# Hybrid attention encoder layer: VectorE jobs made by late ScalarE jobs run a slot later; the mixed rows' squares and low parts within VectorE's budget

## The chip, the cores and the metric

One core of one Trainium2 chip. The metric is the device time of one execution in microseconds (us), smaller is better. A core has TensorE (PE, matrix products; PEld is its weight load), VectorE (DVE), ScalarE (ACT), GpSimd (POOL) and SyncE (SP), each with its own queue that runs in order. Engines wait for each other through semaphores.

## The reference, cut to what matters

The layer reads x of 1024 tokens by 1024 columns. One projection of the normalised x gives queries, keys, values and gates of two groups of heads. Group A is plain attention, group B looks at a neighbourhood on a token grid of 16 rows by 64 columns. Both are gated, put beside each other, projected again and added to x.

```python
h = _rmsnorm(x, norm_gain[l])
proj = h @ w_in[l]
q_a, k_a, v_a, g_a, q_b, k_b, v_b, g_b = jnp.split(proj, split_at, axis=-1)
...
o_a = _gqa_blocked(q_a, k_a, v_a) * jax.nn.silu(g_a)
o_b = _neighbourhood_attn(q_b..., k_b..., v_b..., na_rpb[l])
o_b = o_b * jax.nn.silu(g_b)
mixed = jnp.concatenate([o_a, o_b], axis=-1)
x = x + mixed @ w_out[l]
return _rmsnorm(x, final_norm_gain)
```

The result is float32. The kernel gets near that precision with float16 products by splitting each operand into a high part (rounded to float16) and a low part (what is left), and adding three products: high by high, high by low, low by high.

## The kernel before

**Stages.** First x is normalised, split and transposed (to about 74 us). Then come projections and group A's attention in one loop of units (to about 366 us). Then group B's attention runs in 32 steps, four for each block u of 128 tokens and two heads a step; meanwhile PE also runs the rest of the gate projections and the first part of the output projection. After that the rest of the output projection and the last norm follow, without steps of attention.

**A step of group B** (`fl.step`, called by `run_units`, with `parts_b`). `b_lo` makes the low part of the previous step's probabilities (L845 on DVE) and issues their transpose on SP (L847). `b_qk` puts two heads' scores on PE (L815 and L818, into one of three score banks), takes for each the biased scores and their minimum on DVE (L836), two exponentials on ACT (L838) and a cast to the high part (L840). Then the jobs of DVE are emitted, then about 24 matmuls of projection on PE (`fill`, L494), and last `b_pv`, the product with the values of three steps earlier (L865 to L867). The order in which these calls are made is each engine's order, as the engines are scheduled by hand there.

**Jobs.** Everything else of ACT and DVE is a job. `job(engine, cost, fn, delay, late)` puts one into a list with a first step at which it may run and a class `late`; `work(engine)` takes jobs in the order of (late, first step, number) as long as the engine's budget for the step holds out. A job with `late=0` runs whatever the budget is. `fl.step` calls `work("act")` twice: ahead of `b_qk` for at most 1.2 us of cost (`fl.early`, set only in group B's loop), and behind it for the rest ("late ACT jobs"); `work("dve")` comes behind both. `need` runs jobs at once, out of turn, when PE is about to use their result.

**The jobs that matter here.**
- *Weights.* `load_w(g)` fetches the 1 MB of group g's weights (L212, on POOL's queue). Four steps later `squares` adds up their squares in quarters on ACT (L362); two steps after that PE sums them over the partitions (L378, in `b_scores`), DVE scales the sum (L380) and POOL takes a power (L381). `split` then makes four ACT jobs `hi` (L404) and, from each, a DVE job `lo` (L409, called `wlo` here, group by group). The last `lo` of group g lets group g+2 be loaded at the next step. Groups 13 to 16 are the output projection.
- *Mixed rows.* When a block u has all its heads, `os_start` runs: squares on ACT (`sq`, L902) and then DVE (`scale`, L907), a power on POOL (L910), two ACT jobs `hi` (L915) and two DVE jobs `lo` (L919), and two transposes on SP (L928). These are ready for the output projection.
- *Gates.* The tanh is an ACT job (L694), the product behind it a DVE job (L699); both are made at once, when the projection ends.
- *Values.* DVE divides by the sums (L874 to L877), POOL multiplies by the gate (L879). The output projection is added to x by L976; L1001 squares the result for the last norm.

Of the kernel before, what the change touches and what calls it, by code (L numbers as in the profile page):

```python
# [47 lines left out]
class Flow:  # L48


    def __init__(self):
        self.slot = 0
        self.due = {}
        self.queue = []
        self.credit = 0.0
        self.jobs = []
        self.base = None
        self.budget = {}
        self.left = {}
        self.early = None  # L60

    def at(self, delay, pos, fn, *a):
        self.due.setdefault((self.slot + delay, pos), []).append((fn, a))

    def job(self, eng, cost, fn, *a, delay=1, late=1, key=None):

        self.jobs.append((late, self.slot + delay, self.number(), eng, cost, fn, a, key))

    def need(self, key, done):
# [50 lines left out]
    def step(self, n, first=None, second=None, last=None):  # L120
        if self.base:
            us = self.base[0] + 0.654 * n
            self.budget = {"act": us - self.base[1], "dve": us - self.base[2]}
        self.run("pre")
        self.work("act", self.early)
        if first:
            first()
        if self.early is not None:
            self.work("act", more=True)
        if second:  # L130
            second()
        self.run("mid")
        self.work("dve")
        self.run("post")
        self.fill(n)
        if last:
            last()
        self.run("end")
        self.slot += 1
# [3 lines left out]
def kernel(ctx: ExitStack, tc: tile.TileContext, x: bass.AP, w: bass.AP, wo: bass.AP,  # L143
# [3 lines left out]
    act, dve, pool, pe, sp = nc.scalar, nc.vector, nc.gpsimd, nc.tensor, nc.sync  # L147
# [11 lines left out]
    at, job = fl.at, fl.job  # L159
# [42 lines left out]
    def tn(name, n=1, tag="t"):  # L202
        return tiny.tile([P, n], F32, tag=tag, name=name)


    raw, wp, late, x2 = {}, {}, {}, {}
# [149 lines left out]
    def squares(g, delay):  # L356

        wss[g] = [tn(f"wss{g}_{k}", 1, "ws") for k in range(4)]

        def quarter(i):  # L360
            o = late["r"][0][:, 2048:2560].bitcast(BF16) if "b" in late else va_more
            act.activation(o.rearrange("p (k c) -> p k c", c=GC), raw[g][:, QUARTERS[i]], AF.Square, accum_out=wss[g][i])  # L362
            if i == 3:
                job("act", 0, pend.append, g, delay=2 if "b" in late else 1, late=0, key=("sq", g))
        for i in range(4):
            job("act", 0.75 if g < 13 else 1.0, quarter, i, delay=delay, late=3 if g < 13 else 1.2, key=("sq", g))
# [31 lines left out]
    def split(g):  # L398

        alloc_wp(g)  # L400

        def hi(i):
            q = QUARTERS[i]
            act.activation(wp[g][0][:, q], raw[g][:, q], AF.Copy, scale=col(S_ + g))  # L404
            job("dve", 1.0 if "b" in late else 0.72, lo, i, delay=0, late=0.5 if g > 11 else 2, key=g)

        def lo(i):
            q = QUARTERS[i]
            dve.scalar_tensor_tensor(wp[g][1][:, q], raw[g][:, q], col(S_ + g), wp[g][0][:, q], op0=OP.mult, op1=OP.subtract)  # L409
            if i < 3:  # L410
                return
            ready.add(g)
            prep_e(g)
            if g + 2 < 17:
                at(1, "pre", load_w, g + 2)
            if g > 14:
                t = wraw.tile([P, 2, 1024], F32, tag="raw", name=f"x2{g}")
                for i in range(2):
                    have_x2(ORDER[2 * g - 26 + i], t[:, i])
        for i in range(4):  # L420
            job("act", 0.3 if g == 14 else 0.6, hi, i, late=0.5 if g > 11 else 2, key=g)
# [464 lines left out]
    def mixed(u):  # L886
        return mixA[u // 2][:, u % 2], mixB[u // 2][:, u % 2]

    def os_start(u):

        if not all({("b", u, c), ("a", u // 2, c * GC)} <= ready for c in range(2)):
            at(1, "post", os_start, u)
            return
        t = rws[u] = tn(f"os{u}", 4, "os")
        k = ORDER.index(u)
        hl = one.tile([P, 2, 1024], F16, tag=f"q{k % 2}0" if k > 3 else "gain", name=f"mhl{u}")
        osp[u] = [hl[:, 0], hl[:, 1]]
        ms = mixed(u)
        cs = [slice(i * 512, (i + 1) * 512) for i in range(2)]

        def sq():
            act.activation(late["r"][0][:, 2048:2560].bitcast(BF16), ms[0], AF.Square, accum_out=t[:, 0:1])  # L902
            job("dve", 0.95, scale, delay=0, late=0, key=("os", u))

        def scale():
            junk = late["r"][1][:, 2048:2560] if k else osp[u][0][:, cs[1]]
            dve.tensor_tensor_reduce(out=junk.bitcast(BF16), in0=ms[1], in1=ms[1], scale=1.0, scalar=t[:, 0:1],  # L907
                                     op0=OP.mult, op1=OP.add, accum_out=t[:, 1:2])
            dve.tensor_scalar(t[:, 1:2], t[:, 1:2], 2.0 ** -30, 1e-36, op0=OP.mult, op1=OP.add)
            pool.tensor_tensor(t[:, 2:3], t[:, 1:2], mh[:, :1], op=OP.pow)  # L910
            for i in range(2):
                job("act", 0.72, hi, i, delay=1, late=0, key=("os", u))

        def hi(i):
            act.activation(osp[u][0][:, cs[i]], ms[i], AF.Copy, scale=t[:, 2:3])  # L915
            job("dve", 0.8, lo, i, delay=0, late=0, key=("os", u))

        def lo(i):
            dve.scalar_tensor_tensor(osp[u][1][:, cs[i]], ms[i], t[:, 2:3], osp[u][0][:, cs[i]], op0=OP.mult, op1=OP.subtract)  # L919
            if i:  # L920
                dve.reciprocal(t[:, 3:4], t[:, 2:3])
                os_c(u)
        job("act", 0.82, sq, delay=1, late=0, key=("os", u))

    def os_c(u):
        mT[u] = [m.bitcast(F16).rearrange("p (a b) -> p a b", b=P) for m in mixed(u)]
        for k in range(2):
            sp.dma_start_transpose(mT[u][k], osp[u][k])  # L928
        at(1, "end", turn_x2, u)
# [369 lines left out]
```

## Time and profile before

| what | us |
|---|---|
| median of 3 runs (567.64 to 570.32) | 567.69 |
| the profiled execution, device time | 566.36 |
| its span | 564.5 |
| PE busy | 515.5 (91%) |
| DVE busy | 446.0 (79%) |
| ACT busy | 367.8 (65%) |

The span runs from the first to the last instruction; the other 1.9 us lie around it. Group B's first scores start at 366.1 us and its last at 502.0. In rows of groups, "xcount | busy, mean ns | idle" gives how many instructions there were, their busy time, the mean of one in ns, and how long the engine had been idle ahead of them, with what ended the idle time. In rows of the timeline the first number is the start, the second the duration, both in us.

### The profile page before, as it was taken

How to read it: one execution, taken by the hardware profiler on the slowest of the kernel's cores; microseconds unless marked ns; L12 is line 12 of the kernel's file. 1: busy time of each engine (PE TensorE's matmuls, PEld its weight loads, DVE VectorE, ACT ScalarE, POOL GpSimd, SP SyncE). 2: the span in 40 equal slices, each digit the busy share in tenths (PEclk: the TensorE clock that was granted, in tenths of full speed). 3: DMA queues.
4: the chain of work that ended last, by engine and by line, in shares of the span. 5: the costliest groups of instructions: out<-in, count | busy, mean ns of one | idle time of the engine just before them, and what ended most of it. 6: DMA issues, size and time to landing. Idle time of an engine off the chain costs nothing.

```text
span 564.5 us, 13778 instructions
## 1 busy us (share of the span) xinstructions
PE 515.5 (91%) x5583; PEld 402.4 (71%) x5583; DVE 446.0 (79%) x911; ACT 367.8 (65%) x583; POOL 157.2 (28%) x181
## 2 busy tenths in 40 slices
PE   2577989989999999999999999999998889998994
PEld 0456877767887555568888888887776667788883
DVE  4588788989887988778789887588987798988532
ACT  5546456958787759587696886367777568663211
POOL 2395887670000000000000022433821231224000
PEclk9979999999999999999999999999999998999998
DMA  8999549789999999998999899436586599996612
GB/s 242 220 181 234 122 71 210 125 143 191 203 228 174 175 216 193 193 187 173 211 197 180 189 165 214 129 68 132 105 188 105 117 255 230 181 154 139 215 38 75
DMA packets 244513, 95.47 MB, mean 169 GB/s; under 512 B 235489, under 2 KB 236001, under 8 KB 242530
## 3 DMA queue, kind: packets, MB, share of 16 engines
q1 hardware_dynamic: 240850, 73.89, 71.8%
q0 software_dynamic: 3312, 19.92, 12.2%
q8 instruction: 43, 0.70, 0.5%
q10 hardware_dynamic: 288, 0.79, 0.5%
q14 instruction: 20, 0.16, 0.1%
HBM read 29.56 MB, written 4.19 MB: 60 GB/s over the span
## 4 chain that ended last, share of the span: by engine, by line
PE 51%; DVE 9%; ACT 8%; issue 5%; DMA 4%; SPq 0%; POOL 0%; DVEq 0%; POOLq 0%; ACTq 0%
PE pj L494 19%; PE kb L494 7%; PE pjb L494 5%; PE s L725 4%; PE s L727 4%; ACT rq L838 3%; PE sb L494 3%; PE pv L758 3%; DMA ar<-ar 3%; PE pv L759 3%; PE pv L757 3%; ACT ar L840 3%; DVE ar L836 2%; DVE ar L845 2%; DMA x2b<-in_x_dram 1%
## 5 line engine op out<-in xcount | busy, mean ns | idle before, releaser
L494 PEld LDWEIGHTS <-hT 128*128 128x128 f16 x2112 | 204.9, 100 | 58.8 <-issue 16.2
L494 PE MATMUL pj<-whl,hT 128*128 128x256 f16 x1680 | 201.6, 278 | 20.9 <-DMA hT<-ar 7.8
L734 ACT ACTIVATE ar<-s,nm,sm 128x1024 f32<-128x1024 f32 x64 | 76.9, 1202 | 56.6 <-DVE nm L732 56.3
L732 DVE CUSTOM_DVE_ANT_0 ar<-s,sm 128x1024 bf16<-128x1024 f32 x64 | 82.0, 1281 | 33.9 <-PE s L727 33.6
L494 PEld LDWEIGHTS <-ar 128*128 128x128 f16 x768 | 74.6, 99 | 11.7 <-issue 2.6
L740 DVE TENSOR_TENSOR ar<-ar 128x1024 f16<-128x1024 f32 x64 | 79.5, 1242 | 1.4 <-ACT ar L735 1.4
L735 ACT ACTIVATE ar<-ar 128x1024 f16<-128x1024 f32 x64 | 67.6, 1057 | 2.1 <-DVE sum L764 0.3
L838 ACT ACTIVATE rq<-ar,nm 128x384 f32<-128x384 f32 (+1 forms) x64 | 34.1, 580 | 38.4 <-DVE nm L836 37.7
L494 PE MATMUL pjb<-whl,ar 128*128 128x256 f16 x408 | 47.4, 273 | 0.0
L494 PE MATMUL kb<-hT,whl 128*128 128x512 f16 x192 | 44.5, 379 | 0.0
L409 DVE SCALAR_TENSOR_TENSOR whl<-raw,sm,whl 128x512 f16<-128x512 f32 x52 | 38.7, 770 | 2.8 <-ACT whl L404 2.8
L758 PE MATMUL pv<-va,ar 128*128 128x64 f16 x384 | 40.1, 194 | 0.0
L757 PE MATMUL pv<-va,ar 128*128 128x65 f16 x384 | 40.1, 193 | 0.0
L759 PE MATMUL pv<-va,ar 128*128 128x65 f16 x384 | 39.9, 192 | 0.0
L757 PEld LDWEIGHTS <-ar 128*128 128x128 f16 x384 | 35.7, 97 | 5.5 <-issue 0.3
L758 PEld LDWEIGHTS <-ar 128*128 128x128 f16 x384 | 35.5, 97 | 5.5 <-issue 0.3
L725 PE MATMUL s<-kTa,rq 128*128 128x512 f16 x128 | 38.5, 383 | 0.4 <-ACT ar L734 0.4
L212 POOL DMA_DIRECT2D raw<-in_w_dram x11 | 6.7, 607 | 113.0 <-ACT ar L735 89.0
L845 DVE SCALAR_TENSOR_TENSOR ar<-rq,ar 128x768 f16<-128x768 f32 (+1 forms) x32 | 30.7, 959 | 7.9 <-ACT ar L840 7.5
L879 POOL TENSOR_TENSOR ar<-ar,qkg 128x256 f32<-128x256 f32 x16 | 18.5, 1157 | 65.0 <-DVE qkg L877 63.7
L759 PEld LDWEIGHTS <-ar 128*128 128x128 f16 x384 | 35.5, 99 | 0.0
L404 ACT ACTIVATE whl<-raw,sm 128x512 f16<-128x512 f32 x52 | 34.0, 709 | 1.4 <-POOL sm L381 1.4
(174 smaller groups left out, 978.4 us busy)
## 6 DMA issues: line engine op xcount, KB each, us to landing
raw<-in_w_dram POOLq DMA_DIRECT2D x11, 1024.0 KB, 7.7
raw<-in_wo_dram POOLq DMA_DIRECT2D x4, 1024.0 KB, 6.3
ar<-in_x_dram SPq DMA_DIRECT2D x7, 512.0 KB, 6.3
khh<-ar SPq DMA_DIRECT2D x16, 128.0 KB, 3.4
x2b<-in_x_dram POOLq DMA_DIRECT2D x4, 512.0 KB, 6.9
x<-in_x_dram POOLq DMA_DIRECT2D x4, 512.0 KB, 6.2
out_dram<-x2b SPq DMA_DIRECT2D x8, 256.0 KB, 4.2
out_dram<-x SPq DMA_DIRECT2D x7, 256.0 KB, 2.9
```

The source lines that it names most:

```text
L409: dve.scalar_tensor_tensor(wp[g][1][:, q], raw[g][:, q], col(S_ + g), wp[g][0][:, q], op0=OP.mult, op1=OP.subtract)
L494: pe.matmul(*o[0], **o[1])
L725: pe.matmul(s[:, c * 512:(c + 1) * 512], q, kTa[:, 4 * c:4 * c + 4, hh], start=True, stop=False)
L732: dve.tensor_tensor_reduce(out=hl[:, 1].bitcast(BF16), in0=s, in1=col(SHA).to_broadcast([P, 1024]), scale=col(NSA), scalar=3e38, op0=OP.ad ...
L734: act.activation(p32, s, AF.Exp, bias=nm, scale=col(SCA))
L735: at(0, "mid", lambda: act.activation(hl[:, 0], p32, AF.Copy))
L740: dve.tensor_tensor(hl[:, 1], p32, hl[:, 0], op=OP.subtract)
L757: pe.matmul(o, pt[:, kt], va[:, kt, hh, v_hi], start=kt == 0, stop=False)
L758: pe.matmul(o[:, :D], pt[:, kt], va[:, kt, hh, v_lo], start=False, stop=False)
L759: pe.matmul(o, pt[:, 8 + kt], va[:, kt, hh, v_hi], start=False, stop=kt == 7)
L838: act.activation(p32[:, e], t[:, e], AF.Exp, bias=nm, scale=-1.0)
L845: dve.scalar_tensor_tensor(hl[:, 1], p32, 2.0 ** 14, hl[:, 0], op0=OP.mult, op1=OP.subtract)
```

## The change

A field `lag` holds how many steps later than the current one a new job may run at the earliest. It is 1 while late ACT jobs run and 0 otherwise, so that a job which a late ACT job makes (a DVE `lo` behind its `hi`, above all) can run in the next step at the earliest, and no longer in the same one. And three DVE jobs of the mixed rows are no longer of class 0: the squares `scale` and both `lo` get `late=0.2`, so they count against the budget and stand behind class 0; the cost given for `lo` goes from 0.8 to 0.95.

```diff
@@ class Flow
+        self.lag = 0
...
     def job(self, eng, cost, fn, *a, delay=1, late=1, key=None):
 
+        delay = max(delay, self.lag)
         self.jobs.append((late, self.slot + delay, self.number(), eng, cost, fn, a, key))
@@ def step
         if self.early is not None:
+            self.lag = 1
             self.work("act", more=True)
+            self.lag = 0
@@ def os_start
         def sq():
             act.activation(late["r"][0][:, 2048:2560].bitcast(BF16), ms[0], AF.Square, accum_out=t[:, 0:1])
-            job("dve", 0.95, scale, delay=0, late=0, key=("os", u))
+            job("dve", 0.95, scale, delay=0, late=0.2, key=("os", u))
...
         def hi(i):
             act.activation(osp[u][0][:, cs[i]], ms[i], AF.Copy, scale=t[:, 2:3])
-            job("dve", 0.8, lo, i, delay=0, late=0, key=("os", u))
+            job("dve", 0.95, lo, i, delay=0, late=0.2, key=("os", u))
```

No instruction is added or dropped; the order changes on ACT, DVE, POOL and SP, and on PE only in the place of the weights' sums. Line numbers of the changed kernel are 4 higher from `fl.step` on.

**ACT, steps 14 and 15.** Before, the exponentials and cast of step 14 (`nm_4`, `nm_5`) are followed by three quarters of group 15's squares and the mixed rows' `hi`, then by step 15 (`nm_6`, `nm_7`) and the tanh:

```order
L838 ACTIVATE rq<-ar,nm_4_5938 128x384
L838 ACTIVATE rq<-ar,nm_5_5941 128x384
L840 ACTIVATE ar<-rq 128x768
L362 ACTIVATE rest_5101,wss_0_5670<-raw_5668 128x512
L362 ACTIVATE rest_5101,wss_1_5671<-raw_5668 128x512
L362 ACTIVATE rest_5101,wss_2_5672<-raw_5668 128x512
L915 ACTIVATE mhl_5887<-ar,os_5886 128x512 x2
L838 ACTIVATE rq<-ar,nm_6_6008 128x384
L838 ACTIVATE rq<-ar,nm_7_6011 128x384
L840 ACTIVATE ar<-rq 128x768
L694 ACTIVATE ar<-pjb_5196,sm 128x512
```

The same place in the changed kernel, from the same exponentials to the same tanh:

```order
L842 ACTIVATE rq<-ar,nm_4_5930 128x384
L842 ACTIVATE rq<-ar,nm_5_5933 128x384
L844 ACTIVATE ar<-rq 128x768
L919 ACTIVATE mhl_5879<-ar,os_5878 128x512 x2
L842 ACTIVATE rq<-ar,nm_6_6005 128x384
L842 ACTIVATE rq<-ar,nm_7_6008 128x384
L844 ACTIVATE ar<-rq 128x768
L698 ACTIVATE ar<-pjb_5196,sm 128x512
```

The three squares are gone from here; they now stand in steps 18 and 19.

**DVE, steps 15 and 16.** Before, from the gate product and the sums of step 15 to the minima of step 16 (`nm_0`, `nm_1`) and the next squares:

```order
L699 SCALAR_TENSOR_TENSOR ar<-ar,pjb_5196 128x2x256
L874 RECIPROCAL sumb_1_6017<-pvb_5116 128x4
L875 TENSOR_TENSOR sumb_1_6017<-sumb_1_6017,sm 128x4
L877 TENSOR_TENSOR qkg<-pvb_5116,sumb_1_6017 128x256
L919 SCALAR_TENSOR_TENSOR mhl_5887<-ar,os_5886,mhl_5887 128x512 x2
L921 RECIPROCAL os_5886<-os_5886 128x1
L845 SCALAR_TENSOR_TENSOR ar<-rq,ar 128x768
L836 ISA ar,nm_0_6081<-sb_5113,ar,sm 128x384
L836 ISA nm_0_6081 128x1
L836 ISA ar,nm_1_6084<-sb_5111,ar,sm 128x384
L836 ISA nm_1_6084 128x1
L907 ISA rest_5102,os_6027<-ar,os_6027 128x512
```

The same place in the changed kernel:

```order
L703 SCALAR_TENSOR_TENSOR ar<-ar,pjb_5196 128x2x256
L878 RECIPROCAL sumb_1_6014<-pvb_5116 128x4
L879 TENSOR_TENSOR sumb_1_6014<-sumb_1_6014,sm 128x4
L881 TENSOR_TENSOR qkg<-pvb_5116,sumb_1_6014 128x256
L923 SCALAR_TENSOR_TENSOR mhl_5879<-ar,os_5878,mhl_5879 128x512
L849 SCALAR_TENSOR_TENSOR ar<-rq,ar 128x768
L840 ISA ar,nm_0_6074<-sb_5113,ar,sm 128x384
L840 ISA nm_0_6074 128x1
L840 ISA ar,nm_1_6077<-sb_5111,ar,sm 128x384
L840 ISA nm_1_6077 128x1
L923 SCALAR_TENSOR_TENSOR mhl_5879<-ar,os_5878,mhl_5879 128x512
L925 RECIPROCAL os_5878<-os_5878 128x1
```

One `lo` has moved behind the minima of step 16, and the squares (L911) follow it.

**ACT and DVE, step 28.** Before, ACT has the four `hi` of group 16 in steps 25 and 26, two behind each cast; the first two stand here behind step 25 (`nm_2`, `nm_3`):

```order
L838 ACTIVATE rq<-ar,nm_2_6710 128x384
L838 ACTIVATE rq<-ar,nm_3_6713 128x384
L840 ACTIVATE ar<-rq 128x768
L404 ACTIVATE whl_6301<-raw_6273,sm 128x512 x2
L838 ACTIVATE rq<-ar,nm_4_6780 128x384
L838 ACTIVATE rq<-ar,nm_5_6783 128x384
L840 ACTIVATE ar<-rq 128x768
L404 ACTIVATE whl_6301<-raw_6273,sm 128x512 x2
```

In the changed kernel all four stand behind step 28 (`nm_0`, `nm_1`) on ACT:

```order
L906 ACTIVATE rest_5101,os_6845<-ar 128x512
L842 ACTIVATE rq<-ar,nm_0_6903 128x384
L842 ACTIVATE rq<-ar,nm_1_6906 128x384
L844 ACTIVATE ar<-rq 128x768
L408 ACTIVATE whl_6423<-raw_6403,sm 128x512 x4
L919 ACTIVATE mhl_6846<-ar,os_6845 128x512 x2
```

And on DVE the sum's scale (L384) and all four `wlo` (L413) of group 16 stand in step 28 too:

```order
L849 SCALAR_TENSOR_TENSOR ar<-rq,ar 128x768
L384 TENSOR_SCALAR wss_0_6405<-sb_5111 128x1
L840 ISA ar,nm_0_6903<-sb_5113,ar,sm 128x384
L840 ISA nm_0_6903 128x1
L840 ISA ar,nm_1_6906<-sb_5111,ar,sm 128x384
L840 ISA nm_1_6906 128x1
L911 ISA rest_5102,os_6845<-ar,os_6845 128x512
L911 ISA os_6845 128x1
L913 TENSOR_SCALAR os_6845<-os_6845 128x1
L413 SCALAR_TENSOR_TENSOR whl_6423<-raw_6403,sm,whl_6423 128x512 x4
```

PE's order is the same in both kernels except that the four sums of group 15 (L378) move from step 18 to 21, and those of group 16 from step 25 to 28. Step 28 has 12 matmuls of an earlier tile and then the first 12 with group 16, in both kernels. On POOL the loads of groups 15 and 16 move from steps 10 and 19 to steps 15 and 21.

## The prediction

> **What bounds the kernel.** I read the page first, then the waits, then the stretch in which the change acts, stage by stage.
>
> ```profile
> PE 515.5 (91%) x5583; PEld 402.4 (71%) x5583; DVE 446.0 (79%) x911; ACT 367.8 (65%) x583; POOL 157.2 (28%) x181
> ```
>
> TensorE (PE) does work that the change leaves alone, so the time is PE's work plus PE's gaps. The change acts only in the neighbourhood stage (`fl.early` is set there alone). I number its slots by step: in step s PE starts the scores of pair s with its first L815. Step 14 starts at 420.41 us, step 29 at 492.93, and the slots end at about 502.
>
> ```profile
> 420.41:492.93 72.52, 64.35 (x722) 50.21 (x719) 60.65 (x156) 52.22 (x100) 17.53 (x22) 0.95 0.90 173
> 492.93:502.00 9.07, 8.72 (x106) 6.90 (x102) 8.93 (x26) 5.82 (x10) 2.71 (x3) 1.00 0.78 121
> 502.00:564.50 62.50, 53.49 (x538) 47.32 (x536) 33.80 (x94) 16.24 (x38) 9.99 (x14) 0.96 0.53 124
> ```
>
> In this view of stretches the busy times are PE, PEld, DVE, ACT, POOL, then the granted clock. In steps 14 to 28 PE is busy 64.35 of 72.52 us and VectorE (DVE) 60.65: two engines of nearly the same load, each waiting on the other. PE's gaps, from the timeline:
>
> ```profile
> 391.77 0.27 PE L815 MATMUL sb<-khh,qTb 128*128 128x256 f16 x1 [0.97 <-DVE nm L836]
> 395.71 0.19 PE L865 MATMUL pvb<-rq,ar 128*128 128x65 f16 x1 [0.73 <-DVE qkg L877]
> 419.86 0.19 PE L865 MATMUL pvb<-ar 128*128 128x65 f16 x1 [0.75 <-DVE qkg L877]
> 435.31 0.32 PE L815 MATMUL sb<-khh,qTb 128*128 128x384 f16 x1 [2.33 <-DVE nm L836]
> 447.71 0.32 PE L815 MATMUL sb<-khh,qTb 128*128 128x384 f16 x1 [2.74 <-DVE nm L836]
> 460.41 0.32 PE L815 MATMUL sb<-khh,qTb 128*128 128x384 f16 x1 [0.28 <-DVE nm L836]
> 466.31 0.32 PE L815 MATMUL sb<-khh,qTb 128*128 128x384 f16 x1 [1.88 <-DVE nm L836]
> 489.23 0.32 PE L815 MATMUL sb<-khh,qTb 128*128 128x384 f16 x1 [0.94 <-DVE nm L836]
> 494.91 0.49 PE L494 MATMUL sb<-whl,ar 128*128 128x256 f16 x3 [0.35 <-DVE whl L409]
> 509.90 0.20 PE L865 MATMUL pvb<-rq,ar 128*128 128x65 f16 x1 [1.42 <-DMA ar<-ar]
> ```
>
> The number in brackets is the gap. An L815 waits for a score bank: there are three banks and two heads a step, so the second head of step s needs the first minimum (L836) of step s-1, and that stands in DVE's queue behind the jobs of step s-2. The five such gaps from 435.31 to 489.23 sum to 8.17 us. Two of them cost more than their length:
>
> ```profile
> 432.73:436.14 3.41, 1.08 (x11) 0.41 (x8) 3.41 (x8) 0.78 (x2) 0.51 (x1) 1.00 0.63 144
> 436.14:439.56 3.42, 3.42 (x18) 2.46 (x17) 3.38 (x9) 3.39 (x7) 1.01 (x1) 0.50 0.65 125
> 442.97:446.38 3.41, 2.00 (x31) 1.66 (x30) 3.34 (x8) 0.00 (x0) 1.16 (x1) 1.00 0.03 7
> 446.38:449.80 3.42, 2.09 (x18) 1.50 (x18) 3.24 (x10) 2.01 (x4) 1.10 (x2) 1.00 0.97 165
> 463.45:466.86 3.41, 1.53 (x26) 0.86 (x24) 3.41 (x10) 0.50 (x1) 1.25 (x2) 1.00 1.15 230
> 466.86:470.28 3.42, 3.42 (x19) 2.42 (x18) 2.57 (x6) 3.16 (x8) 0.00 (x0) 0.50 1.15 238
> ```
>
> Cut into stretches of 3.41 us, one in which PE is busy 1.08 or 1.53 us is followed by one at clock 0.50; 2.00 and 2.09 us busy, the longest gap split over two stretches, is not. A half-clock stretch loses 3.42 x 0.5 = 1.7 us of matmul. The Trainium skill ("TensorE: Matmul & The Clock Gate", Part 1 on the clock gate) has the clock halve only after a whole idle window of about 3.4 us; here gaps of 1.88 and 2.33 us did it, so the rows decide. By that rule both 1.7s below fall away and so does the one that I add, and the sum would come to some 2 us worse, still inside "no change".
>
> **Part 1: ScalarE (ACT) is lighter in steps 14 to 17.** The lag and the 0.2 move single `wlo` and `lo` jobs later, so group 13 is split at step 14 instead of 9, the load of group 15 starts at step 15 instead of 10, and its squares (L362) leave ACT at step 14.
>
> ```profile
> 426.06 0.63 ACT L362 ACTIVATE rest<-raw 128x512 bf16<-128x512 f32 x1
> 426.68 1.32 ACT L915 ACTIVATE mhl<-ar,os 128x512 f16<-128x512 f32 x2
> 430.50 0.69 DVE L699 SCALAR_TENSOR_TENSOR ar<-ar,pjb 128x512 f32<-128x512 f32 x1 [3.62 <-ACT ar L694]
> 442.21 0.67 ACT L694 ACTIVATE ar<-pjb,sm 128x512 f32<-128x512 f32 x1
> 442.91 0.69 DVE L699 SCALAR_TENSOR_TENSOR ar<-ar,pjb 128x512 f32<-128x512 f32 x1 [2.97 <-ACT ar L694]
> ```
>
> In step 15 DVE's gate product (L699) waited 3.62 us for the tanh (L694), which stood behind three squares, two `hi` and the exponentials. Tanh and gate product are not jobs of the edited kind: the product still stands in the step of its tanh, right behind the minima. What is left is the way minimum, two exponentials, cast, tanh. With the durations below that is 2.05 + 0.6 us from the first minimum's end, less 0.55 for the second minimum, so a DVE wait of 2.1 us. The gain on that wait is 1.5 us, on the 2.97 some 0.9.
>
> ```profile
> L845 DVE SCALAR_TENSOR_TENSOR ar<-rq,ar 128x768 f16<-128x768 f32 (+1 forms) x30 | 28.8, 959 | 6.4 <-ACT ar L840 6.0
> L836 DVE CUSTOM_DVE_ANT_0 ar<-sb,ar,sm 128x384 f32<-128x384 f32 (+1 forms) x32 | 17.3, 575 | 0.5 <-DMA ar<-ar 0.5
> L409 DVE SCALAR_TENSOR_TENSOR whl<-raw,sm,whl 128x512 f16<-128x512 f32 x16 | 11.6, 745 | 2.8 <-ACT whl L404 2.8
> L919 DVE SCALAR_TENSOR_TENSOR mhl<-ar,os,mhl 128x512 f16<-128x512 f32 x12 | 11.3, 979 | 0.0
> L838 ACT ACTIVATE rq<-ar,nm 128x384 f32<-128x384 f32 (+1 forms) x60 | 31.9, 578 | 34.0 <-DVE nm L836 33.3 <-ACT ar L694 0.6
> L840 ACT ACTIVATE ar<-rq 128x768 f16<-128x768 f32 (+1 forms) x30 | 23.6, 786 | 1.0
> L404 ACT ACTIVATE whl<-raw,sm 128x512 f16<-128x512 f32 x16 | 10.6, 707 | 0.0
> ```
>
> Second, one `lo` (L919, 0.98 us) leaves step 15 and both leave step 17. The first minimum of step 16 then follows the tanh by product 0.6, sums 0.77, one `lo` 0.93, low part (L845) 0.9, minimum 0.6 = 3.8 us. Followed by hand from step 14, it ends at 433.4 instead of 435.25, and PE waits 0.5 instead of 2.33. **Gain 1.8 us, and 1.7 for the half clock behind it.** In step 17 the tanh is behind two `hi` of weights, two of a row and the exponentials as before: I get waits of 0.65 and 1.6 at steps 18 and 19 for the 2.74: **gain 0.5**. Bounds of these three: 0 (the row unchanged) and 8.5 (2.33 + 2.74 + both half clocks).
>
> **Part 2: steps 20 to 27.** DVE's jobs are evened out: the heavy steps had two `lo` (1.96) beside two adds and the sums. But DVE's work to step 28 is the same 60.65 us to within one job, and what leaves one step arrives in the next. By hand I get 0.25, 0.45, 0.85, 0.5 and 1.2 us of waits against 0.28 + 1.88 + 0.94 = 3.1: **0**, bounds -2 and +3. None of mine is as long as 1.88, so the half clock at 466.86 goes: **gain 1.7**. On POOL the two 1 MB loads (L212) move behind the row scales (L910) and some loads of x (L966), and so lie beside the transposes of steps 15 to 17 and 21 to 23. I price that at 0, since PE there waits for DVE anyway; a transpose that comes too late would cost about what one did at 509.90, 1.4. Steps 3 to 13 lose or gain single `lo` jobs beside running matmuls: 0, bounds -0.5 and 0.5.
>
> **Part 3: the last weights come too late.** Every later split delays the next load. Group 14 ends at step 20 instead of 18, group 16 is loaded at 21 instead of 19, squared at step 25, and its sums stand on PE in step 28 instead of 25. But PE multiplies with group 16 in the same step 28, behind only 12 other matmuls. So scale, four ACT `hi` and four DVE `lo` run while PE waits, behind the step's own scores.
>
> ```profile
> 476.62 0.34 PE L818 MATMUL sb<-klo,qTb 64*128 64x384 f16 x2
> 476.88 0.25 PE L378 MATMUL sb<-wss,mh 128*128 128x1 bf16 x4
> 477.00 2.67 PE L494 MATMUL pjb<-whl,ar 128*128 128x256 f16 x23
> 478.13 0.15 DVE L380 TENSOR_SCALAR wss<-sb 128x1 f32<-128x1 f32 x1
> 478.37 0.54 POOL L381 TENSOR_TENSOR sm<-wss,mh 128x1 f32<-128x1 f32 x1 [1.16 <-DVE wss L380]
> 480.86 1.32 ACT L404 ACTIVATE whl<-raw,sm 128x512 f16<-128x512 f32 x2
> ```
>
> These rows are the same steps for group 16 in the kernel before, at step 25. If PE reaches step 28 waiting for DVE, DVE still has the second minimum 0.55, adds 0.8, sums 0.75, low part 0.9 and the next minimum 0.6 ahead = 3.6; then exponentials and cast 2.05, `hi` 0.66, `lo` 0.77: 7.1 us. PE has 0.6 of scores and 12 x 0.11 = 1.3 of matmuls: it waits 5.2. If PE isn't held there the same way gives 3.0. With four squares and an L1001 (5 x 0.7) ahead of the exponentials of step 26, DVE is late; I take 5.0, bounds 3.0 and 6.5. Behind the waiting L494 stand the values' matmuls (L865 to L867) of step 28 and the scores of 29, so all of PE is held. POOL's power (0.54) is hidden by the exponentials. Behind the gap comes a half clock: a gap of 5 leaves one 3.41 us stretch at least 2.5 us idle, more than the 1.88 above; I take 1.4 of 1.7, as part of it can fall into the gap. The 0.35 at 494.91 goes. **Loss 5.0 + 1.4 - 0.35 = 6.05.**
>
> **Part 4: the end.** The pause lets DVE and ACT catch up, and the last row transposes (L928) now stand one L847 later on SP.
>
> ```profile
> 499.32 2.62 SPq L928 DMA_TRANSPOSE ar<-mhl  x2
> 502.11 6.85 SPq L847 DMA_TRANSPOSE ar<-ar  x2
> ```
>
> The L847 at 502.11 stood behind the two L928 and held PE 1.42 us at 509.90; now it goes ahead of them: **gain 1.4**, bounds 0 and 1.4. From there PE runs on without a gap, and its order of rows is the same.
>
> **Sum.** Gains 1.8 + 1.7 + 0.5 + 0 + 1.7 + 1.4 = 7.1, loss 6.05: about 1.0 us faster. The first three gaps (0.97, 0.73, 0.75) stay. The profiled execution took 566.36 us (span 564.5), so 565.3; the median of the runs shown is 567.69, 1.3 above it, so **566.7** for a median.
>
> **Rivals.**
> - *DVE evens out fully.* With DVE's load below PE's in every step but 28, the gaps of steps 15 to 28 sink to 1.5, so 8.17 + 3.4 - 1.5 = 10.1 gained, against 3.7 + 1.4 - 0.35 = 4.75, plus 1.4: 6.7 us faster, 561.0. For it: counted with the durations above, no step but 28 has over 5.1 us of DVE work any more, where steps 15, 17, 21, 25 and 29 had 5.7 to 6.1. Against: 6.0 us of L845's idle are waits for the cast L840, which the change doesn't shorten. 0.30.
> - *Group 16 decides (slower).* Its gap reaches 6.5 with two half-clock stretches behind it (3.4, as a 6.5 us gap can empty two), and steps 15 to 27 give only 3.3: 3.3 - 9.55 + 0.4 = 5.9 slower, 573.6. It decides from a gap of about 6 us on. Against: it needs DVE over a step behind at 28. 0.17, with milder forms from 570.5 on.
> - *No effect.* The lag touches only jobs made by late ACT jobs; tanh and gate product, which made the two longest waits, keep their order, so gaps only change place: 567.7. 0.08.
>
> My forecast itself has 0.45. A measurement of this kernel tells about 0.5%, 2.8 us, from no change. Forecast and "no effect" lie within it: same 0.53, faster 0.30, slower 0.17. The range leaves out the far half of the first rival's lower end and the worst of the second: 560.5 to 571.5; the forecast's own is 563.5 to 570.
>
> **What would show it.** Right: L699's wait in step 15 near 2 us; no gap of 2 us at steps 17 to 27; one gap of 4 to 6 us at an L494 behind L408 or L413 in step 28 and clock 0.50 after it; no DMA wait of 1.4 us at the last L869. Wrong: gaps above 2 us before step 28, a gap under 3 there, or a new wait of PE on a transpose while groups 15 and 16 load.

## The result, and the profile after

The changed kernel takes 577.45 us in the median (568.79 to 589.43), the one before 569.57 beside it (565.97 to 578.61). The ratio is 1.0068, 95% interval 1.004 to 1.0097: slower by 0.7%, some 3.9 us, where 566.7 and "no change" were forecast. The ratio counts only executions within 1.5% of the shortest of their kernel (10 of 20 here, 17 of 20 before) and the median counts all, which is why the medians lie further apart.

The profiled execution took 576.46 us (span 574.7), 10.1 more than that of before. These two lie far apart: 566.36 is near the shortest of the kernel before (565.97), and 576.46 is the longest of the ten that the ratio counts here. What follows dates these 10.1 us; the typical loss is the ratio's 3.9. The line of busy times on its page:

```profile
PE 519.0 (90%) x5583; PEld 403.8 (70%) x5583; DVE 446.2 (78%) x911; ACT 367.9 (64%) x583; POOL 157.7 (27%) x181
```

DVE and ACT work as before; PE is busy 3.5 us longer with the same matmuls, by half clocks, and the rest of the 10.1 are gaps. PE's waits from step 15 on, from the timeline (start, duration, instruction, and in brackets the gap ahead and what ended it):

```profile
434.08 0.32 PE L819 MATMUL sb<-khh,qTb 128*128 128x384 f16 x1 [0.66 <-DVE nm L840]
438.29 0.32 PE L819 MATMUL sb<-khh,qTb 128*128 128x384 f16 x1 [0.18 <-DVE nm L840]
446.46 0.32 PE L819 MATMUL sb<-khh,qTb 128*128 128x384 f16 x1 [4.14 <-DVE nm L840]
462.05 0.20 PE L869 MATMUL pvb<-ar 128*128 128x65 f16 x1 [2.11 <-DMA ar<-ar]
470.42 0.20 PE L869 MATMUL pvb<-ar 128*128 128x65 f16 x1 [4.32 <-DMA ar<-ar]
483.10 2.68 PE L498 MATMUL pjb<-whl,ar 128*128 128x256 f16 x23 [1.15 <-DVE whl L413]
494.43 0.32 PE L819 MATMUL sb<-khh,qTb 128*128 128x384 f16 x1 [0.21 <-DVE nm L840]
500.81 0.37 PE L498 MATMUL sb<-whl,ar 128*128 128x256 f16 x1 [4.27 <-ACT whl L408]
501.60 2.51 PE L498 MATMUL sb<-whl,ar 128*128 128x256 f16 x11 [0.41 <-DVE whl L413]
```

Three places stand out: 4.14 in step 19 on a minimum, 2.11 and 4.32 in steps 21 and 22 on a transpose of the probabilities, 4.27 + 0.41 in step 28 on group 16's weights. The last L869 has no gap any more. The first L815 or L819 of a step on PE's timeline dates the loss:

| | step 14 | step 20 | step 23 | step 28 | step 29 | last step | end of span |
|---|---|---|---|---|---|---|---|
| before, us | 420.41 | 452.07 | 464.11 | 487.97 | 492.93 | 501.83 | 564.5 |
| after, us | 420.84 | 452.49 | 470.97 | 493.90 | 504.90 | 513.54 | 574.7 |
| after minus before | 0.43 | 0.42 | 6.86 | 5.93 | 11.97 | 11.71 | 10.2 |

Up to step 20 nothing is won or lost. Steps 20 to 22 lose 6.4, steps 23 to 27 win back 0.9, step 28 loses 6.0, the end gains 1.5.

**Step 19.** ACT's timeline shows why the minimum came late:

```profile
436.02 1.32 ACT L408 ACTIVATE whl<-raw,sm 128x512 f16<-128x512 f32 x2
439.74 1.33 ACT L919 ACTIVATE mhl<-ar,os 128x512 f16<-128x512 f32 x2 [2.40 <-DMA ar<-mhl]
440.98 1.10 ACT L842 ACTIVATE rq<-ar,nm 128x384 f32<-128x384 f32 x2
442.12 0.84 ACT L844 ACTIVATE ar<-rq 128x768 f16<-128x768 f32 x1
442.87 0.67 ACT L698 ACTIVATE ar<-pjb,sm 128x512 f32<-128x512 f32 x1
```

The `hi` of the third row stood still for 2.40 us, and the exponentials and the tanh (L698) behind it. The first four row blocks share one buffer (`mhl`, tag "gain"). Its last readers are the transposes of the row before, and these are issued only when that row's second `lo` is done, which the change moved one step later. SP's timeline, before and after:

```profile
432.74 2.59 SPq L928 DMA_TRANSPOSE ar<-mhl  x2
```

```profile
435.10 2.99 SPq L932 DMA_TRANSPOSE ar<-mhl  x2
```

In before they went out 2.4 us earlier and L915 did not wait. From the tanh the delay goes on to DVE's queue: product, sums, low part, minimum.

```profile
443.57 0.69 DVE L703 SCALAR_TENSOR_TENSOR ar<-ar,pjb 128x512 f32<-128x512 f32 x1 [4.79 <-ACT ar L698]
445.79 0.61 DVE L840 CUSTOM_DVE_ANT_0 ar<-sb,rq,sm 128x384 f32<-128x384 f32 x1
```

**Steps 21 and 22.** SP's timeline and, in the view of the tile `ar` from 453 to 475 us, the transposes' time from issue to landing:

```profile
447.63 5.61 SPq L932 DMA_TRANSPOSE ar<-mhl  x2
453.36 20.18 SPq L851 DMA_TRANSPOSE ar<-ar  x4
```

```profile
DMA to landing us min/median/max: 5.5/8.6/15.5
```

The same view of before, 447 to 469 us, has 2.8/6.8/8.2. POOL's loads lie in the same stretch:

```profile
446.40 0.60 POOL L970 DMA_DIRECT2D x2b<-in_x_dram  x1
453.55 0.58 POOL L970 DMA_DIRECT2D x2b<-in_x_dram  x1
457.54 0.55 POOL L970 DMA_DIRECT2D x2b<-in_x_dram  x1
458.09 0.57 POOL L216 DMA_DIRECT2D raw<-in_wo_dram  x1
465.91 0.60 POOL L970 DMA_DIRECT2D x2b<-in_x_dram  x1
```

Group 16's 1 MB (L216) stands behind the third load of x; before, L212 was issued at 450.08, behind the first.

**Step 28.** The sums of group 16 stand in this step (in the kernel before at 476.88, in step 25), and PE's wait for its high parts (500.81 above) follows them:

```profile
494.95 0.25 PE L382 MATMUL sb<-wss,mh 128*128 128x1 bf16 x4
495.07 1.47 PE L498 MATMUL pjb<-whl,ar 128*128 128x256 f16 x12
```

### The profile page after: what moved, and what is told of

The parts are those of the page before. It is cut to its first block, busy times and chain, and to the rows that moved or that the text cites. A ratio compares the mean times of both kernels' runs of the same rounds, so it can differ in the third digit from the quotient of the medians.

```text
span 574.7 us, 13778 instructions
## 1 busy us (share of the span) xinstructions
PE 519.0 (90%) x5583; PEld 403.8 (70%) x5583; DVE 446.2 (78%) x911; ACT 367.9 (64%) x583; POOL 157.7 (27%) x181
## 4 chain that ended last, share of the span: by engine, by line
PE 53%; DVE 8%; ACT 7%; issue 5%; DMA 4%; SPq 1%; POOL 0%; DVEq 0%; POOLq 0%; ACTq 0%
PE pj L498 18%; PE kb L498 7%; PE pjb L498 6%; PE s L731 4%; PE s L729 4%; DMA ar<-ar 4%; PE sb L498 3%; PE pv L762 3%; ACT rq L842 3%; PE pv L763 3%; PE pv L761 3%; DVE ar L840 2%; ACT ar L844 2%; DVE ar L849 1%; ACT rest L366 1%
## 5 line engine op out<-in xcount | busy, mean ns | idle before, releaser
L413 DVE SCALAR_TENSOR_TENSOR whl<-raw,sm,whl 128x512 f16<-128x512 f32 x52 | 38.5, 770 | 1.3 <-ACT whl L408 1.3
L216 POOL DMA_DIRECT2D raw<-in_w_dram x11 | 6.7, 607 | 112.8 <-ACT ar L739 89.0
L408 ACT ACTIVATE whl<-raw,sm 128x512 f16<-128x512 f32 x52 | 33.9, 708 | 1.4 <-POOL sm L385 1.4
```

## The experiments

Theories, each for one of the gaps. **R**: the row buffer holds ACT (step 19). **L**: loads beside transposes slow them (steps 21 and 22). **W**: group 16's weights come too late (step 28). A rival to all: one backlog that is paid wherever PE waits first. All results in one table; gaps are those of PE's timeline in the one profiled execution of each, "before" is the kernel before on the same chip.

| kernel | median us (runs: lowest to highest) | before, us | ratio, 95% interval | step 19 | transposes, steps 21, 22 | weights, step 28 |
|---|---|---|---|---|---|---|
| changed | 577.45 (20: 568.79 to 589.43) | 569.57 | 1.0068, 1.004 to 1.0097 | 4.14 | 2.11 + 4.32 | 4.68 |
| after_again | 579.04 (12: 567.74 to 585.68) | 567.04 | 1.0049, 1.0004 to 1.0094 | 4.13 | 2.35 + 16.06 | 4.68 |
| x_later | 571.71 (12: 566.81 to 581.15) | 567.23 | 1.0056, 1.0023 to 1.009 | 4.15 | 4.05 + 3.33 | 4.79 |
| sq_early | 573.85 (12: 566.07 to 580.61) | 567.23 | 1.0013, 0.9965 to 1.0062 | 4.12 | 1.83 | 2.83 |
| row_buf | 568.38 (12: 565.34 to 576.96) | 567.23 | 1.0017, 0.9991 to 1.0042 | 1.69 | 2.10 | 4.68 |
| all3 | 565.54 (12: 561.39 to 570.8) | 567.23 | 0.9964, 0.9932 to 0.9996 | 1.70 | 2.29 | 2.02 |
| lag_only | 576.2 (4: 572.23 to 577.07) | 567.63 | 1.0104, 1.005 to 1.0159 | 3.83 | 6.92 | 4.12 |
| late_only | 578.51 (4: 576.23 to 583.44) | 567.63 | 1.017, 1.0111 to 1.023 | 2.08 | 2.76 + 8.27 | 4.47 |
| no_w16 | 570.75 (10: 569.0 to 577.43) | 567.63 | 1.0081, 1.004 to 1.0122 | 4.15 | 1.45 | 4.70 |
| best1 | 565.62 (12: 560.04 to 573.59) | 567.63 | 0.9926, 0.9886 to 0.9965 | 1.69 | 2.46 | 0 |
| w16_later | 571.52 (12: 567.4 to 582.13) | 567.04 | 1.0047, 1.0007 to 1.0088 | 4.13 | 3.06 + 1.99 | 4.79 |
| best2 | 564.95 (12: 559.73 to 566.9) | 567.04 | 0.9946, 0.991 to 0.9983 | 1.70 | 2.33 | 0 |
| loads_apart | 573.6 (6: 569.34 to 578.13) | 567.85 | 1.0114, 1.0063 to 1.0165 | 4.13 | 3.44 | 4.68 |
| before_w16 | 569.41 (12: 565.27 to 575.1) | 567.85 | 1.003, 0.9991 to 1.0068 | 3.03 | 0 | 0 |
| row_cut | 577.9 (6: 571.22 to 587.18) | 568.18 | 1.0129, 1.006 to 1.0198 | 4.14 | 2.75 + 6.23 | 4.69 |
| row_buf_again | 568.48 (12: 565.97 to 573.93) | 568.18 | 1.0034, 0.9996 to 1.0072 | 1.69 | 2.17 | 4.68 |

### One cause at a time

**Loads of x later** (changed kernel):

```diff
-X2_BEHIND = {0: (0, 1), 1: (2,), 2: (3,), 3: (4,), 4: (5,), 5: (6,), 6: (7,)}
+X2_BEHIND = {0: (0, 1), 3: (2,), 4: (3, 4), 5: (5,), 6: (6, 7)}
```

> The changed kernel, with the loads of x for the third to eighth block (L970) asked for one to three row blocks later, so that only one 0.5 MB load and group 16's 1 MB stand beside the transposes of steps 19 to 22. Theory L (loads bunch and slow the transposes L851): the two PE waits at L869 on a transpose (2.11 and 4.32 us) go to under 1 us together, the half clock behind them (1.7) goes too, L851 lands in under 10 us where it took 15.47; 6 to 8 us less than the changed kernel. The gaps in step 19 (4.14) and step 28 (4.27 + 0.41) stay. Rival (the transposes are late because DVE hands their rows over late, or group 16's 1 MB alone does it): waits of over 4 us at L869 stay and the time with them.

Missed: the waits on transposes are 4.05 + 3.33, 7.4 us together where they were 6.4. The median is lower, but the ratio is nearly that of the changed kernel (1.0056). The later loads of x, as far as this edit moves them, were not the cause of these waits.

**Group 16's squares two steps earlier:**

```diff
-            squares(g, 4)
+            squares(g, 2 if g == 16 else 4)
```

> The changed kernel, with the four squares of group 16 two steps after its load instead of four, so that its sums stand on PE in step 25 instead of 28; nothing else is edited. Theory W (group 16's weights come too late): the PE wait in step 28 (4.27 + 0.41) goes to under 1 us and the half clock behind it (3.4) goes; 5 to 8 us less than the changed kernel; the gaps of steps 19 and 21/22 stay. Rival (the wait in step 28 is where DVE's and ACT's backlog is paid off, whoever is waited for): as much comes back as waits for the minima (L840) in steps 25 to 30, and the time changes by under 2 us. Squares that wait for the load (it landed at 470.61) would hold ACT in step 22 or 23.

W in direction, not in size (ratio 1.0013, some 3 us less than the changed kernel, where 5 to 8 were expected): the sums stand in step 25, and PE's timeline has one gap left in step 28.

```profile
493.87 1.23 PE L498 MATMUL sb<-whl,ar 128*128 128x256 f16 x5 [2.83 <-DVE whl L413]
```

The waiting moved from ACT's `hi` (L408) to the last three `wlo`, which the planner still puts behind the row's jobs, into step 28. The step lasts 7.78 us instead of 11.00. In this execution the 4.32 of step 22 is missing too, although the program is the same up to there.

**A buffer of its own for the third row's high part** (two free 1 KB pieces; so its first transpose is cut in two):

```diff
+        halves = [t[:, 2560:3072] for t in late["r"]] if k == 2 else [hl[:, 0, :512], hl[:, 0, 512:]]
...
-            act.activation(osp[u][0][:, cs[i]], ms[i], AF.Copy, scale=t[:, 2:3])
+            act.activation(halves[i], ms[i], AF.Copy, scale=t[:, 2:3])
...
+            if halves and k == 0:
+                for i in range(2):
+                    sp.dma_start_transpose(mT[u][0][:, 4 * i:4 * i + 4], halves[i])
```

> The changed kernel, with the high part of the third row block (L919, the one of step 16) in memory of its own, so that it need not wait for the transposes of the second one; its first transpose is cut in two. Theory R (reuse of the row buffer holds ACT): the ACT wait of 2.4 us before L919 goes, the tanh (L698) follows 2.4 us earlier, the PE gap of step 19 falls from 4.14 to about 1.8 us and the half clock behind it (1.7) may go: 2 to 4 us less. Rival (the minimum of step 19 is held by DVE's own queue): the gap stays over 3.5 us. The gaps of steps 21/22 and 28 stay.

R holds for step 19. ACT's timeline, with no wait ahead of the row's `hi` (now L920):

```profile
436.36 1.32 ACT L408 ACTIVATE whl<-raw,sm 128x512 f16<-128x512 f32 x2
437.63 1.33 ACT L920 ACTIVATE rest<-ar,os 128x512 f16<-128x512 f32 x2
...
440.76 0.67 ACT L698 ACTIVATE ar<-pjb,sm 128x512 f32<-128x512 f32 x1
```

The gap is 1.69. By the ratios (1.0017 against 1.0068) the kernel is some 2.9 us shorter, within the 2 to 4 expected. What was not expected: the 4.32 of step 22 is gone as well, and the median falls by some 9 us, as the longest executions are gone too (576.96 at most, where the changed kernel had 589.43).

**All three:**

> All three edits together: later loads of x, early squares of group 16, a row buffer of its own. If L, W and R are separate causes, their gains add to 13 to 18 us against the changed kernel, and the kernel is 4 to 8 us faster than the one before. If they are one backlog that is paid at whichever place comes first, the sum falls well short, under 10 us against the changed kernel.

The median is 565.54, 1.7 below the kernel before, ratio 0.9964; less than forecast, since 2.29 on a transpose, 2.02 on `wlo` and two waits on transposes at the end (0.41 and 0.90) are left. The test set beforehand does not decide between separate causes (13 to 18 us less than the changed kernel) and one backlog (under 10): by the medians, on two chips, it is 11.9, by the profiled spans 9.7, by the ratios some 6. What speaks against one backlog are the gaps: those of steps 19 and 28 fell with their own edits, and none came back elsewhere at full size.

### The two halves of the change

**The lag alone** (the rows' jobs as before):

```diff
-            job("dve", 0.95, scale, delay=0, late=0.2, key=("os", u))
+            job("dve", 0.95, scale, delay=0, late=0, key=("os", u))
...
-            job("dve", 0.95, lo, i, delay=0, late=0.2, key=("os", u))
+            job("dve", 0.8, lo, i, delay=0, late=0, key=("os", u))
```

> The lag alone: the rows' squares and low parts keep cost and place of the kernel before (late 0, 0.8). Both low parts of a row stand in one step again, so the transposes of the second row start as early as before. Theory R: L919 of step 16 doesn't wait for them and the PE gap of step 19 is 2.7 us or less (4.14 in the changed kernel). Theory W: group 16's sums stand one step earlier than in the changed kernel (27, not 28), which is still too late: PE waits 2.5 to 4.5 us in step 28. Together 3 to 6 us less than the changed kernel, near the kernel before. If the lag is the whole harm, the time is that of the changed kernel.

**The class alone** (`self.lag = 1` is left out):

> The lower class (0.2) and cost of the rows' jobs alone, without the lag. Weights of groups 13 to 15 keep the steps of before; the row's low parts move by one step here and there, but not the ones ahead of step 16's L919. Theory R: no wait of L919 in step 16, gap of step 19 2.7 us or less. Theory W: group 16's sums stand in step 28 as in the changed kernel, so the PE wait of 4 to 5 us there is whole, with its half clock: 3 to 5 us slower than before. If the class is harmless and the lag does the harm, the time is that of before.

Either half alone is slower, by 1.0% and 1.7% (four executions each). W holds in both (4.12 and 4.47 in step 28). L919 waited in neither, as R says, but with the lag alone the gap of step 19 is 3.83, not 2.7: DVE has both `lo` of the row (1.87) ahead of the minimum.

```profile
443.92 1.87 DVE L923 SCALAR_TENSOR_TENSOR mhl<-ar,os,mhl 128x512 f16<-128x512 f32 x2
...
446.64 0.60 DVE L840 CUSTOM_DVE_ANT_0 ar<-sb,rq,sm 128x384 f32<-128x384 f32 x1
```

Before had this order too; there PE itself came 1.5 us later (444.65 against 443.15), since it had run at half clock. With the class alone the pause is 3.52 in step 17. Behind either pause PE waited long for transposes in step 22:

```profile
471.56 0.23 PE L869 MATMUL pvb<-ar 128*128 128x65 f16 x1 [6.92 <-DMA ar<-ar]
```

```profile
475.00 0.23 PE L869 MATMUL pvb<-ar 128*128 128x65 f16 x1 [8.27 <-DMA ar<-ar]
```

### What slows the transposes

**The changed kernel again:**

> The changed kernel once more, unedited, beside the others on one chip: 572 to 579 as a median, a spread of over 10 us. If waits on transposes in steps 21 and 22 make the spread, this execution's span differs from the 574.7 of the first profile by what those waits differ from 6.4 us (and the half clock behind them), and steps 19 (4.1) and 28 (4.7) are the same to 0.2 us.

This execution was 9.2 us longer than the first profiled one, by its timeline for one reason:

```profile
444.05 0.48 PE L819 MATMUL sb<-khh,qTb 128*128 128x384 f16 x1 [4.13 <-DVE nm L840]
460.95 0.20 PE L869 MATMUL pvb<-ar 128*128 128x65 f16 x1 [2.35 <-DMA ar<-ar]
481.05 0.24 PE L869 MATMUL pvb<-ar 128*128 128x65 f16 x1 [16.06 <-DMA ar<-ar]
```

Step 19 is the same to 0.01 us, step 28 too; the wait of step 22 is 16.06 instead of 4.32, and up to step 14 this execution was 2.4 us ahead. The wait differs from execution to execution of one program, and it made this one long.

**Without group 16's load:**

```diff
-        pool.dma_start(raw[g], w[g] if g < 13 else wo[g - 13])
+        if g == 16:
+            pool.memset(raw[g], 0.02)
+        else:
+            pool.dma_start(raw[g], w[g] if g < 13 else wo[g - 13])
```

> The changed kernel without the load of group 16 (its 1 MB is filled with a constant by POOL; the last 256 columns of the projection are so left out). Theory L, in the form left by the later loads of x (group 16's 1 MB beside the transposes of steps 19 to 22 slows them): the two waits at L869 on a transpose in steps 21 and 22 (2.11 and 4.32, with 1.7 of half clock) fall under 1 us together, transposes there land in under 9 us, and the spread of the runs shrinks from 20 us to under 10; 5 to 8 us less. Rival (after the pause of step 19 the rows' and the steps' transposes bunch by themselves): a wait of 2 us or more stays there, and the spread stays. Gaps of steps 19 and 28 stay.

One wait of 1.45 is left, and the executions spread over 8.4 us (10 of them) instead of 20.6 (20). That speaks for L; but the ratio is no better than the changed kernel's (1.0081).

**The same load two steps later** (squares two steps behind it):

```diff
-                at(1, "pre", load_w, g + 2)
+                at(3 if g == 14 else 1, "pre", load_w, g + 2)
...
-            squares(g, 4)
+            squares(g, 2 if g == 16 else 4)
```

> The changed kernel, with the load of group 16 two steps later (23 instead of 21) and its squares two steps behind it instead of four, so that squares, sums and everything behind them keep their places. Nothing is left out and no byte less is moved. Theory L (the 1 MB beside the transposes of steps 19 to 22 slows them): as without the load, the waits at L869 in steps 21 and 22 sum to under 2 us, the median falls by 4 to 7 us against the changed kernel. Rival (the constant fill only took bytes out of a stage that is short of DMA time): the waits move to steps 23 and 24, where the load now lies, and the median falls by under 2 us. Steps 19 (4.1) and 28 (4.7) stay.

The median falls as L says (571.52 against 579.04 on the same chip), but the ratio does not (1.0047 against 1.0049), and the waits stay at 3.06 + 1.99.

**Both edits to the loads:**

> The changed kernel, with both edits to the loads: group 16's 1 MB two steps later and the loads of x for the third block on one to three rows later, so that in steps 20 to 22 only the second 0.5 MB load of x stands beside transposes. Theory L (bytes loaded beside transposes decide): the waits at L869 in steps 21 and 22 sum to under 2.5 us, no run is above 573 us, and the median is 567 to 570. Rival P (the pause of step 19 and the transposes that come out of it in a row are enough): stalls of over 4 us and runs above 575 remain. Steps 19 (4.1) and 28 (4.7) stay.

With one 0.5 MB load beside the transposes PE still waited 3.44, and executions of 575.73 and 578.13 remain. L in this form falls: taking the loads away is not enough.

**The load's new place in the kernel before** (the diff of w16_later, applied to before):

> The kernel before, with group 16's load two steps later (21, behind the third load of x, where the changed kernel has it) and its squares two steps behind it instead of four; all else on PE, DVE, ACT and SP as before. Theory L: waits of PE on transposes appear in steps 21 to 23, the median rises by 3 us or more and the spread grows beyond 12 us. Rival P: no such waits, the time is that of the kernel before within 1.5 us.

Between both: 1.6 us slower in the median, ratio 1.003 with 1 in its interval, and two short waits on transposes, in steps 24 and 25.

```profile
472.68 0.20 PE L865 MATMUL pvb<-rq,ar 128*128 128x65 f16 x1 [1.35 <-DMA ar<-ar]
477.46 0.20 PE L865 MATMUL pvb<-ar 128*128 128x65 f16 x1 [0.60 <-DMA ar<-ar]
```

So the load alone is worth a small part at most, not clear of the noise. The own row buffer had done more than all edits to the loads, but it had also cut a transpose. Apart:

**The cut alone** (pieces of the old buffer, so that L919 waits):

```diff
-        halves = [t[:, 2560:3072] for t in late["r"]] if k == 2 else [hl[:, 0, :512], hl[:, 0, 512:]]
+        halves = [hl[:, 0, :512], hl[:, 0, 512:]]
```

> The changed kernel, with the first transpose of the third row cut in two as in the kernel of the own row buffer, but in the old buffer, so that L919 of step 16 waits as before. Theory P (the pause of step 19 brings the stalls): gap of step 19 about 4.1 us, waits at L869 in steps 21 and 22 as in the changed kernel (2 to 16 us, 4 or more in most executions), median 574 to 580 and a spread over 12 us. Rival C (the cut, that is one more and shorter entry in SP's queue, ends the stalls): median 568 to 572, few runs above 575, with the gap of step 19 still there.

**The own buffer once more:**

> The kernel with the row buffer of its own once more, beside row_cut on one chip: both theories expect 567 to 570 as a median and few runs above 574, with a gap of 1.7 us in step 19 and a wait of about 2.1 us on a transpose in step 21.

On one chip 577.9 against 568.48 in the median; by the ratios, 1.0129 and 1.0034, some 5.4 us, from few executions (six and twelve) and with intervals that overlap a little. With the cut alone, PE's timeline is that of the changed kernel:

```profile
443.16 0.48 PE L819 MATMUL sb<-khh,qTb 128*128 128x384 f16 x1 [4.14 <-DVE nm L840]
459.91 0.20 PE L869 MATMUL pvb<-ar 128*128 128x65 f16 x1 [2.75 <-DMA ar<-ar]
471.85 0.24 PE L869 MATMUL pvb<-ar 128*128 128x65 f16 x1 [6.23 <-DMA ar<-ar]
```

So it is the wait for the buffer, with the pause that it makes, and not the cut. (That the pieces lie in other memory was not tried by itself.) The table points the same way over all kernels: the ten with a pause of 3.5 us or more in step 17 or 19 waited 1.45 to 18.4 us for transposes in steps 21 and 22; the six without one (with the kernel before, seven) never waited more than 2.46. This is one execution of each kernel, the limit of 3.5 was drawn afterwards, and two of the ten (1.45 and 1.83) waited less than 2.46: a pause does not always bring a long wait. Four of the ten profiles are of long executions (after_again, x_later, w16_later, row_cut). Loads may add to how bad it gets behind a pause: with fewer of them the medians lie some 4 to 8 us lower, but the ratios (1.0047 to 1.0114) are no better. That the pause makes the transposes late is therefore likely and not shown, and why it would is open.

### A version that beats both

**Row buffer, early squares, and group 16's low parts first:**

```diff
-            job("dve", 1.0 if "b" in late else 0.72, lo, i, delay=0, late=0.5 if g > 11 else 2, key=g)
+            job("dve", 1.0 if "b" in late else 0.72, lo, i, delay=0, late=(0.1 if g == 16 else 0.5) if g > 11 else 2, key=g)
```

> The changed kernel with the row buffer of its own, early squares of group 16, and that group's low parts ahead of the rows' (0.1 instead of 0.5); loads of x as in the changed kernel. W: what was left in step 28 with early squares (2.02 to 2.83 us behind L413) goes to under 1, as two of the four low parts then stand in step 26. R as measured (step 19: 1.7). Waits on transposes at the end (0.41 and 0.90 with the later loads of x) go. 1 to 3 us less than all three edits: 562 to 565, so 0.5 to 1% faster than before. If waits move on to the next step, it is no better than that kernel (565.5).

Ratio 0.9926 (0.9886 to 0.9965): faster than before by 0.7% and than the changed kernel by 1.4%, some 8 us, by the ratios (12 in the median). Step 28 has no gap. Not as expected: new waits on transposes at the end.

```profile
505.44 0.20 PE L869 MATMUL pvb<-rq,ar 128*128 128x65 f16 x1 [1.21 <-DMA ar<-ar]
517.28 0.20 PE L869 MATMUL pvb<-ar 128*128 128x65 f16 x1 [1.51 <-DMA ar<-ar]
```

**The same with the loads of x elsewhere:**

```diff
+X2_BEHIND = {0: (0, 1), 3: (2, 3, 4, 5), 5: (6,), 6: (7,)}
```

> The kernel of the own row buffer, the early squares and group 16's low parts first (565.6), with the loads of x for the third to eighth block put where few transposes wait: the third to sixth at steps 23 to 26, behind group 16's 1 MB, the last two behind the sixth and seventh row. Theory L: the waits on transposes in step 21 (2.46) and behind the last step (1.21 and 1.51) fall to under 2 us together, 2 to 4 us less: 562 to 564. Rival (they follow the row transposes L937 in SP's queue, whatever is loaded): they stay and so does the time.

Missed: the waits at the end go, but one of 1.92 on a transpose comes in step 28 and the 2.33 of step 21 stays, so the rival is right about step 21. 564.95, not to be told from the 565.62 of the one above, but its slowest execution took 566.9 where that one's took 573.59.

## Why the prediction was wrong

- **Part 1, right in step 17.** The gate product of step 15 waited 2.26 us for its tanh, where "near 2" was expected; the gap of step 17 was forecast at 0.5 and is 0.66, and the half clock behind it is gone.
- **Part 1, wrong in step 19: the step that failed first.** For steps 18 and 19 I worked out 0.65 + 1.6; it is 0.18 + 4.14, and a half clock follows. The chain from tanh to minimum was followed right: with the buffer wait removed (row_buf) the gap is 1.69, and steps 14 to 19 take 27.53 us, where the kernel before takes 31.66 and the changed one 31.65: 4.1 won, as forecast (4.0). What I left out is the buffer. I had moved the row's `lo` and with it its transposes (L932), but asked of them only who reads their result, not who writes next into what they read. So 1.8 + 1.7 + 0.5 of gain became 0.0, by the starts of step 20. In the view of stretches, as PE's busy time and clock:

```profile
444.00:447.41 3.41, 0.95 (x7) 0.49 (x7) 3.34 (x10) 0.91 (x2) 1.92 (x2) 1.00 0.06 14
447.39:450.80 3.41, 3.41 (x18) 2.37 (x17) 3.41 (x8) 2.56 (x6) 0.00 (x0) 0.50 1.01 190
```

- **Part 2, wrong in size.** The loads beside the transposes were priced at 0, "since PE there waits for DVE anyway", a late transpose at 1.4. It was 2.11 + 4.32 and a half clock, in other executions up to 18.4. The named doubt, a new wait of PE on a transpose while group 16 loads, is what came. But the load that I had named is not enough to make it: with group 16's load moved or left out the ratios are no better, and its place by itself costs at most a little (before_w16, ratio 1.003 with 1 in its interval). The long waits went with the buffer wait of step 19 instead (row_cut against row_buf_again, some 5.4 us by the ratios); how the one makes the other stays open. The 1.2 that I had by hand as the longest wait in these steps is near the 1.15 of step 25, but that one is for group 15's low part (L413), and I had named no step, so the likeness may be chance.
- **Part 3, right in the wait and its cause; the agreement of the totals is luck.** Wait 5.0 forecast, 0.21 + 4.27 + 0.41 measured; loss 6.05 forecast, 6.04 by the starts of steps 28 and 29. But the 6.04 has the 0.94 already taken off that the kernel before waited in this step, which Part 2 had counted, and the half clock cost 2.1 (PE busy 6.11 us in the step, 4.02 before) where I took 1.4: it filled two stretches, not one:

```profile
498.59:502.00 3.41, 0.77 (x4) 0.37 (x4) 2.05 (x6) 3.37 (x7) 1.58 (x2) 0.50 1.08 212
502.00:505.42 3.42, 3.42 (x30) 2.44 (x28) 2.63 (x6) 1.82 (x3) 0.55 (x1) 0.50 0.48 83
```

- **Part 4, right.** 1.4 forecast, 1.5 by the last step and the end of the span; the L851 stand ahead of the two L932 on SP now, and the wait is gone.
- **What weighed most.** In the profiled execution the forecast missed by 11 us: 4.0 in Part 1 and 7.2 in Part 2 (1.7 forecast as a gain, 5.5 lost in steps 20 to 27). By the ratio the loss is 3.9, so some 4.9 were missed, and most of that is the 4.0 of Part 1: the gap of step 19 is within 0.02 us of 4.14 in every profile of the changed kernel and of the edits to its loads, while the waits of steps 21 and 22 differ each time.
- **The rivals.** The slower one had the right sign and nearly the right time (573.6; by the ratio 567.69 x 1.0068 = 571.6), for another reason: it asked for a gap of 6 us or more in step 28, which was 4.9, and the rest was lost in steps 19 to 22. The range was too narrow because Part 2's unknown was bounded by -2 and +3, for which no row was named, and in the kernel before PE waits for no transpose in those steps.

## What to carry to other kernels

When a job moves later, follow the buffers it frees as well as the results it makes: a ring of one turns a delay of one step into a wait on an engine that the change never touched. A stage in which PE needs transposes soon after they are issued, with large loads in flight beside them, has no price of 0; bound it by its worst landing, and read several executions, since the same program lost 6 us there in one and 18 in another. And when the last user of late data stands at a fixed place, as group 16's matmuls do in step 28, a delay upstream turns into a wait there; early squares and one priority, with the row buffer, took it away.

## What the runs showed of the hardware

Over the whole kernel, the 80 transposes of `ar` land in a median of 4.5 us. In steps 20 to 22 the slowest took 15.5 us and, in the longest profiled execution, 28.6 (its view of the tile `ar`, 450 to 482 us):

```profile
DMA to landing us min/median/max: 4.2/7.3/28.6
```

Loads were late there too: in that window the 1 MB of group 16 landed in 23.7 us, where loads of its kind take 6.2 in the median of the first profile. The DMA engines count as busy meanwhile and move little. The view of stretches from 461 to 466 us (the last two numbers are the DMA share and GB/s), where that stall begins (PE waits from 465 to 481), first that execution, then the kernel with the own row buffer, which is some 2.4 us further in its program at that time:

```profile
461.00:466.00 5.00, 3.99 (x46) 2.96 (x46) 4.68 (x12) 3.19 (x5) 1.72 (x2) 1.00 1.43 75
```

```profile
461.00:466.00 5.00, 4.35 (x51) 3.40 (x50) 4.89 (x12) 3.45 (x7) 1.71 (x2) 1.00 1.10 341
```

A share of 1.43 at 75 GB/s stands against 1.10 at 341. These are far ends: in the 15 us behind it the first execution moved 126 to 167 GB/s at shares of 0.95 to 1.21. The Trainium skill ("DMA: Bandwidth & Descriptors", Rules for kernel authors) says that a transpose next to ordinary DMAs needs nothing. That rule speaks of right results, and no run here speaks against it; of time it says nothing, and a transpose that took 28.6 us in place of 4.5 is not explained by it.
